# Modulation products on VectorE, a shorter block substitution, paired key products and a gate bound behind solve steps

## The chip, the cores and the metric

The kernel runs on one core of a Trainium2 chip. A core has a matrix engine (TensorE, PE in the profile, with its weight loads shown as PEld), a vector engine (VectorE, DVE), an engine for activations (ScalarE, ACT), a general one (GpSimd, POOL) and a queue engine (SyncE, SP), which here issues most of the transfers. The metric is the time on the device in microseconds of one execution, lower is better.

## The reference, cut to what matters

Two blocks follow each other on 256 tokens of width 1024, all in float32. The first has two layers (a mixer of banded attention and a gated scan, then a mixer with three groups of four scan heads). The second has two layers, each a mixer with a gated delta rule and a sparse attention, and a feed-forward: dense in layer 0, eight experts in layer 1. What the change touches:

```python
mod = c_act @ w_ada[l] + b_ada[l]            # one row of 1024 times 1024 x 6144
sh_m, sc_m, g_m, sh_f, sc_f, g_f = split(mod, 6)
h = rms_norm(x, norm_mix[l]) * (1.0 + sc_m) + sh_m
proj = h @ w_in[l]                           # q, k, v, z, ..., m_g (2048 wide)
...
kb = kc * bc[..., None]                      # delta rule, 8 heads of 64
lower = where(strict, einsum('nbhcd,nbhsd->nbhcs', kb, kc) * decay, 0.0)
tinv = triangular_solve(eye + lower, eye, lower=True, unit_diagonal=True)
...                                          # o_a from tinv, v, decay
gate_a, gate_b = split(sigmoid(m_g), 2)
y = (gate_a * y_a + gate_b * y_b) @ w_out[l]
x = x + g_m * y
```

## The kernel before, in words

**Weights.** Every projection goes through `lin_fm` (line 263, columns of the weight on the output's partitions) or `lin_tm` (277). For each block of 256 columns `wload` (210) loads a raw tile `wr` of 1 MB by a transfer on SP's queue (two buffers), and `wtile` (223) splits it in two halves of 128x1024: ACT writes the high part `wh`, DVE the remainder `wl` (three buffers each). `mm3` (256) then issues three matmuls a product: high by high, high by low, low by high. A block with eight row tiles is 48 matmuls, into one of three PSUM buffers `pl`; an epilogue (`epi`) empties it. `pm` has two PSUM buffers and `pn` three.

**The order.** The program is written once, engine by engine order is made by a planner that lists the instructions by its estimate of when each is ready, with the program's order as rank. So matmuls of a later projection can fill waits of an earlier chain, as far as buffers allow; buffers are handed out in program order. `behind(ins, prev)` orders an instruction after another one on the same engine without a semaphore.

**The stages.** `layer_ab` (0 to some 230 us), `layer_c` (to 525), mixer 0 (to some 838), `ffn_dense` (to some 1100), mixer 1 (to 1378 and the last product with `w_oa_2`), `moe` (to the end).

**Modulation.** For layer 0 of the second block, `ada` (713) makes one of six rows of 1024 per call: eight loads `adaw` of 512 KB on SP's queue (two buffers), 32 matmuls of the column `c_act` against them, in four column groups side by side (64 records in the trace, since a float32 matmul shows as two), an addition of the bias and a transfer on POOL's queue to `modd` in DRAM. `layer_c` calls it at its start (460) and between two projections of its third head group (510), mixer 0 at its start (846), twice ahead of the gates (882) and once behind them (900). `prep_mod` (769) reads rows of `modd` back. For layer 1, `ada_dve` (738) makes the rows on DVE, as chunks behind the weight splits of `ffn_dense`.

**Mixer.** `mixer` (833) projects to `tm`, then queries, keys, values and `z`; `nsa` and `heads` are the sparse attention (their score products `nkT`,`nqT` are written in pairs of heads); `delta` (909) prepares the delta rule. Its loop over eight heads (951 to 979) builds the decays `dd`, multiplies keys by keys and queries (`p0` for the first 128 tokens, `p_1` for the second, on the 64 partitions of a head), and DVE writes them with factors into `UA0` and `UA1` (tiles `dUA`). The 16x16 diagonal blocks go by transfers to `Ub`, 15 pairs of small DVE operations invert them (985 to 989, tiles `dtp` and `dWb`), transfers on ACT's queue lay them out (991 to 996), and `inv32` (1009) makes inverses of 32x32, one half at a time (tiles `dtf`, `dul`, `dys`). `solve` (1027) then goes through eight steps of 32 tokens. A step subtracts the products of all earlier steps' results `X` with the blocks of the key products and multiplies by the inverse:

```python
if T == 0:   # steps 0 to 3
    lst.append((A0(h)[0:32 * cc, 1, r], X[0:32 * cc, 0, xc]))
else:        # steps 4 to 7
    lst.append((A0(h)[:, 1, 128 + 32 * cc:160 + 32 * cc], X[:, 0, xc]))
    if cc:
        lst.append((UA1[0:32 * cc, h, 1, r], X[0:32 * cc, 1, xc]))
```

(per head h; line 1058). Behind the solve in program order stand `gate(1)` and `gate(0)` (897, 898; 1024 columns each, four blocks), the projections `w_ob_2` (901) and `w_oa_2` (906). The planner moves the gates' matmuls ahead of and between the steps of the solve.

Of the kernel before, what the change touches and what calls it, by code (L numbers as in the profile page):

```python
# [89 lines left out]
class Net:  # L90
    def __init__(self, ctx, tc, a, out, dump=None):
# [9 lines left out]
        self.hook = self.hold = None  # L101
# [161 lines left out]
    def lin_fm(self, X, w, c0, ncols, KT, epi):  # L263
# [189 lines left out]
    def layer_c(self):  # L453
        nc, tc, a = self.nc, self.tc, self.a
        with ExitStack() as cx:
# [4 lines left out]
            self.ada()  # L460
# [23 lines left out]
            for gr in range(3):  # L484
# [24 lines left out]
                if gr == 2:  # L509
                    self.ada()  # L510
# [188 lines left out]
    def ada_init(self):  # L699
# [5 lines left out]
        self.ada_next, self.par, self.hook = 0, {}, None  # L705
# [5 lines left out]
        self.modd = [self.dp.tile([6, 4, 256], F32, name="modd%d" % l) for l in range(2)]  # L711

    def ada(self, n=1):

        nc = self.nc
        for _ in range(n):
            r = self.ada_next
            self.ada_next += 1
            w = self.a["w_ada_2"][0]
            ps = self.pl.tile([128, 512], F32, name="pl")  # L720
            o = self.ada_bias(self.aw, 0, r)
            for k in range(8):
                raw = self.aw.tile([128, 1024], F32, name="adaw")
                nc.sync.dma_start(out=raw, in_=w[k * 128:k * 128 + 128, r * 1024:(r + 1) * 1024])
                for j in range(4):
                    self.mm(ps[32 * j:32 * j + 32, :256], self.cs[:, k:k + 1].to_broadcast([128, 32]),
                            raw[:, j * 256:(j + 1) * 256], k == 0, k == 7)
            self.tt(o, o, ps[:, :256], OP.add)
            nc.gpsimd.dma_start(out=self.modd[0][r], in_=o[0::32, :])
# [103 lines left out]
    def mixer(self, l):  # L833
        nc, tc, a = self.nc, self.tc, self.a
        with ExitStack() as cx:
# [9 lines left out]
            if l == 0:  # L845
                self.ada()
# [34 lines left out]
            if l == 0:  # L881
                self.ada(2)
            mg = [p0.tile([128, 8, 256], F32, name="mg%d" % i, tag=("dq", "mg")[i]) for i in range(2)]

            def gate(i):
                self.lin_fm(X, w, 3368 + i * 1024, 1024, 8, lambda m, ps: self.sig(mg[i][:, m:m + 2, :], ps))
# [11 lines left out]
            gate(0)  # L898
            if l == 0:
                self.ada()  # L900
# [8 lines left out]
    def delta(self, l, p1, p2, dq, dv, tm, z):  # L909

        nc, tc, a = self.nc, self.tc, self.a
        c = self.c
# [38 lines left out]
        for h in range(8):  # L951
            hp, r = h // 2, slice(64 * (h % 2), 64 * (h % 2) + 64)
            gt = p2.tile([128, 2, 128], F32, name="dgt")
            for T in range(2):
                self.ts(gt[:, T, :], c["gt"], g[:, T, h:h + 1], None, OP.mult)
            pe = self.pm.tile([128, 4, 128], F32, name="pm")
            self.mm(pe[:, 0:2, :], gt[:, 0, :], c["le1"].rearrange("p (a b) -> p a b", a=2), True, False, **f)
            self.mm(pe[:, 1, :], g[:, 1, h:h + 1].to_broadcast([128, 128]), le, False, False, **f)
            self.mm(pe[:, 2, :], gt[:, 1, :], le, False, False, **f)
            self.mm(pe[:, 0, :], self.identb, self.negst, False, False, **f)  # L960
            self.mm(pe[:, 2, :], self.identb, self.negst, False, True, **f)
            dd = p2.tile([128, 3, 128], F32, name="ddd")
            self.act(dd, pe[:, 0:3, :], AF.Exp)
            p0 = self.pm.tile([128, 2, 256], F32, name="pm")
            p_1 = self.pm.tile([128, 2, 128], F32, name="pm")
            k = dq[r, 4 + hp, :]
            self.mm(p0, k[:, 0:128], dq[r, hp::4, :])
            self.mm(p_1, k[:, 128:256], dq[r, hp::4, 128:256])
            d0 = dd[:, 0:2, :].rearrange("p a b -> p (a b)")
            self.stt(A0(h), p0, be[:, 0, h:h + 1], d0[:, None, :].to_broadcast([128, 2, 256]), OP.mult, OP.mult)  # L970
            self.stt(UA1[:, h], p_1, be[:, 1, h:h + 1], dd[:, 2:3, :].to_broadcast([128, 2, 128]), OP.mult, OP.mult)

            bd = p1.tile([128, 2, 8, 16], F32, name="dbd")
            for T in range(2):
                self.tt(bd[:, T], U(h, T).rearrange("p (b j) -> p b j", j=16), b16, OP.mult)
            nc.vector.tensor_reduce(out=cb[:, :, h], in_=bd.rearrange("p t b j -> p t j b"), op=OP.add, axis=AX)
            for T in range(2):
                q = 64 * T + 8 * h
                nc.gpsimd.dma_start(out=Ub[q:q + 8].rearrange("p s j -> p (s j)"), in_=cb[:, T, h, :])
# [47 lines left out]
    def solve(self, p1, p2, dv, z, A0, UA1, W32, dn, b64, inv32):  # L1027
# [9 lines left out]
        X = p1.tile([128, 2, 512], F32, name="dX", tag="dv")  # L1037
        Rt = p1.tile([128, 512], F32, name="dRt", tag="cbl")
        for n in range(8):
# [8 lines left out]
            for q in range(2):  # L1048
                cq = slice(q * 256, q * 256 + 256)
                src = V[:, 0, :]  # L1050
                if n:
                    for h in range(4 * q, 4 * q + 4):
                        xc = slice(h * 64, h * 64 + 64)
                        lst = []
                        if T == 0:
                            lst.append((A0(h)[0:32 * cc, 1, r], X[0:32 * cc, 0, xc]))
                        else:
                            lst.append((A0(h)[:, 1, 128 + 32 * cc:160 + 32 * cc], X[:, 0, xc]))
                            if cc:
                                lst.append((UA1[0:32 * cc, h, 1, r], X[0:32 * cc, 1, xc]))  # L1060
                        for i, (lh, rh) in enumerate(lst):
                            self.mm(pq[q][r, (h % 4) * 64:(h % 4) * 64 + 64], lh, rh, i == 0, i == len(lst) - 1)
                    self.tt(Rt[r, cq], V[r, T, cq], pq[q][r, :], OP.subtract)
                    src = Rt
                for h in range(4 * q, 4 * q + 4):
                    xc = slice(h * 64, h * 64 + 64)
                    self.mm(pq[q][r, (h % 4) * 64:(h % 4) * 64 + 64], W32[r, T * 8 + h, :], src[r, xc])
# [243 lines left out]
    def ffn_dense(self, l, Y):  # L1311
        nc, tc, a = self.nc, self.tc, self.a
        with ExitStack() as cx:
# [4 lines left out]
            self.tags = {}  # L1318
            mod, scf = self.prep_mod(l, 2, 4, 1)
# [585 lines left out]
```

## Time and profile before

| what | value |
|---|---|
| three runs | 2429.27, 2436.19, 2440.11 us, median 2436.19 |
| the profiled execution | 2426.55 us, span from first to last instruction 2424.7 us |
| mean granted TensorE clock | 0.975 of full |
| PE busy | 2298.4 us, 95% of the span |
| DVE busy | 1565.7 us, 65% |
| ACT busy | 1282.5 us, 53% |
| POOL busy | 388.7 us, 16% |

Busy shares are means over stages with different limits. Matmuls are pipelined, so the time of one record overlaps the next: a record of 0.28 us may follow 0.12 us after the one before it. The clock is given as a share of 2.4 GHz; 0.50 is 1.2 GHz.

### The profile page before, as it was taken

The numbers are of one execution on the slowest core, as the hardware profiler recorded it, in microseconds if no ns is written. First come the engines' busy times: TensorE is split into PE (matmuls) and PEld (weight loads), VectorE is DVE, ScalarE is ACT, GpSimd is POOL, SyncE is SP. The second block draws the span as 40 slices with busy tenths as digits, with TensorE's granted clock in tenths as the row PEclk, the third lists the DMA queues.
The fourth block names the chain that finished last, engine by engine and source line by source line (L and its number), as shares of the span: only waits on it lengthen the run. The fifth ranks groups of instructions, "written<-read, shape, count | busy, mean of one in ns | idle before, by whom it ended". The sixth has DMA issues, their size and how long they took to land. (4 is left out here: it accounts for less than half of the span.)

```text
span 2424.7 us, 40558 instructions
## 1 busy us (share of the span) xinstructions
PE 2298.4 (95%) x15959; PEld 1875.3 (77%) x15959; DVE 1565.7 (65%) x2353; ACT 1282.5 (53%) x1944; POOL 388.7 (16%) x358
## 2 busy tenths in 40 slices
PE   8998999989999899999999999999899999999987
PEld 7887888878678799998878788888788888644333
DVE  5855877757763667676965369998888888511011
ACT  4654666546554444445755258778677867410010
POOL 3201221221110100001110022322331234000000
PEclk9999999989999999999999699999999999999999
DMA  6455446454444578875323358889898999999997
GB/s 202 152 136 162 157 138 205 146 186 135 152 143 140 169 261 282 274 269 156 112 66 106 130 201 323 329 304 363 319 333 323 352 333 337 370 377 408 408 408 317
DMA packets 275192, 586.92 MB, mean 242 GB/s; under 512 B 30752, under 2 KB 171296, under 8 KB 262704
## 3 DMA queue, kind: packets, MB, share of 16 engines
q1 hardware_dynamic: 260688, 577.28, 66.8%
q0 software_dynamic: 5504, 5.91, 1.4%
q8 instruction: 127, 2.08, 0.3%
q10 hardware_dynamic: 8800, 1.05, 0.3%
q14 instruction: 73, 0.60, 0.1%
HBM read 582.26 MB, written 1.64 MB: 241 GB/s over the span
## 5 line engine op out<-in xcount | busy, mean ns | idle before, releaser
L152 DVE TENSOR_TENSOR wl<-wr,wh 128x1024 fp32r<-128x1024 f32 (+3 forms) x733 | 886.3, 1240 | 310.8 <-ACT wh L149 303.6
L149 ACT ACTIVATE wh<-wr 128x1024 fp32r<-128x1024 f32 (+3 forms) x792 | 773.2, 1006 | 414.5 <-PE pl L172 204.6
L172 PE MATMUL pl<-xTh,wh 128*128 128x256 f32 x1696 | 483.5, 286 | 11.1 <-ACT wh L149 5.2
L172 PE MATMUL pl<-xTh,wl 128*128 128x256 f32 x1696 | 480.0, 285 | 0.1
L172 PE MATMUL pl<-xTl,wh 128*128 128x256 f32 x1696 | 479.5, 283 | 0.5 <-DVE xTl L158 0.5
L172 PE MATMUL pl<-wh,eg 128*128 128x448 f32 x1280 | 373.5, 369 | 2.3 <-ACT es L149 2.3
L172 PEld LDWEIGHTS pl<-xTh,wh 128*128 128x128 f32 x1696 | 322.1, 190 | 23.4 <-issue 8.8
L172 PEld LDWEIGHTS pl<-xTl,wh 128*128 128x128 f32 x1696 | 322.5, 190 | 8.0 <-issue 6.8
L172 PEld LDWEIGHTS pl<-xTh,wl 128*128 128x128 f32 x1696 | 321.3, 190 | 6.7 <-issue 5.3
L155 POOL TENSOR_TENSOR wl<-wr,wh 128x896 fp32r<-128x896 f32 (+1 forms) x59 | 189.9, 3219 | 490.3 <-ACT wh L149 383.5
L172 PEld LDWEIGHTS pl<-wh,eg 128*128 128x128 f32 x1280 | 242.4, 190 | 25.0 <-ACT es L149 3.4
L172 PE MATMUL pl<-wl,eg 128*128 128x448 f32 x640 | 238.0, 372 | 14.4 <-POOL wl L155 12.8
L172 PE MATMUL pl<-wr,egf 128*64 128x448 f32 x768 | 163.5, 550 | 3.1 <-DMA wr<-in_w_moe_dram 2.7
L172 PEld LDWEIGHTS pl<-wl,eg 128*128 128x128 f32 x640 | 121.4, 190 | 32.1 <-POOL wl L155 16.9
L172 PEld LDWEIGHTS pl<-wr,egf 128*64 128x64 f32 x768 | 57.8, 137 | 85.6 <-issue 69.7
L172 PE MATMUL pn<-wl,eah 128*128 128x512 f32 x280 | 112.6, 402 | 5.6 <-DVE wl L152 4.1
L172 PE MATMUL pn<-wh,eal 128*128 128x512 f32 x280 | 110.2, 393 | 0.0
L168 DVE TENSOR_SCALAR esu<-pl 128x448 f32<-128x448 f32 x24 | 20.3, 919 | 123.2 <-PE pl L172 123.2
L149 ACT ACTIVATE ehf<-pm 128x448 f32<-128x448 f32 x12 | 6.5, 543 | 168.8 <-PE pn L172 152.0
L172 PE MATMUL pn<-wr,ehf 128*64 128x512 f32 x336 | 89.9, 620 | 5.0 <-DMA wr<-in_w_moe_dram 3.6
L172 PE MATMUL pn<-wh,eah 128*128 128x512 f32 x280 | 89.9, 394 | 0.0
L149 ACT ACTIVATE es<-pl 128x448 f32<-128x448 f32 x64 | 56.9, 989 | 57.8 <-PE pl L172 57.5
(626 smaller groups left out, 3711.9 us busy)
## 6 DMA issues: line engine op xcount, KB each, us to landing
wr<-in_w_moe_dram SPq DMA_DIRECT2D x256, 896.0 KB, 7.0
wr<-in_w_moe_dram SPq DMA_DIRECT2D x96, 1024.0 KB, 8.3
wr<-in_w_dense_dram SPq DMA_DIRECT2D x42, 1024.0 KB, 7.0
wr<-in_w_in_dram SPq DMA_DIRECT2D x32, 1024.0 KB, 5.2
wr<-in_w_in_c_dram SPq DMA_DIRECT2D x30, 1024.0 KB, 5.2
adaw<-in_w_ada_dram SPq DMA_DIRECT2D x48, 512.0 KB, 4.4
adar<-in_w_ada_dram SPq DMA_DIRECT2D x48, 512.0 KB, 5.6
wr<-in_w_in_ab_dram SPq DMA_DIRECT2D x16, 1024.0 KB, 5.3
```

Source lines behind the costliest of these rows:

```text
L149: return self.nc.scalar.activation(out, in_, f, **k)
L152: return self.nc.vector.tensor_tensor(out=out, in0=a, in1=b, op=op)
L155: return self.nc.gpsimd.tensor_tensor(out=out, in0=a, in1=b, op=op)
L168: return self.nc.vector.tensor_scalar(out, a, s1, None, op0=op0)
L172: return self.nc.tensor.matmul(out=out, lhsT=l, rhs=r, start=start, stop=stop, **k)
```

## The change

Four edits.

1. The six modulation rows of layer 0 are made on DVE, by a generator `ada_first` in place of `ada`: 96 chunks of 128x512, each a load of 256 KB and one DVE operation into `adacc`. One chunk is taken up behind the first split of every weight tile from the start of `ada_init` on; what is left is issued at the start of `ffn_dense`. After the 16 chunks of a row, four matmuls with ones (8 records) sum over the partitions.
2. The loop over heads in `delta` goes by pairs: the `p0` products of two heads are issued one after the other, on partitions 0 to 63 and 64 to 127 and into two PSUM tiles, then their `p_1` products.
3. The products with `A0` of steps 4 to 7 of the solve are made once, behind step 3, as eight products of 128x128x64 that are subtracted from `V[:, 1]`.
4. The first matmul of each of the four blocks of `gate(0)` is ordered behind the last matmul of the solve's steps 3, 4, 5 and 6 (the third to the sixth, n = 2 to 5), in both mixers.

```diff
@@ wtile
+            if self.hook0 and k == 0:
+                self.ada_prev = iv
+                next(self.hook0, None)
@@ mm3
-        self.mm(out, ah, bh, start, False, skip_group_check=True)
+        i = self.mm(out, ah, bh, start, False, skip_group_check=True)
+        self.behind(i, self.mm_after)
+        self.mm_after = None
@@ lin_fm(self, X, w, c0, ncols, KT, epi, after=())
+                        if k0 + k == m == 0 and after:
+                            self.mm_after = after.pop(0)
@@ layer_c, mixer: each self.ada() is removed
@@ ada_init
+        self.hook0, self.ada_prev = self.ada_first(), None
+    def ada_first(self):
+        w, o0 = self.a["w_ada_2"][0], None
+        for r in range(6):
             o = self.ada_bias(self.aw, 0, r)
+            acc = self.aw.tile([128, 1024], F32, name="adacc", bufs=1)
             for k in range(8):
+                for h in range(2):
+                    raw = self.aw.tile([128, 512], F32, name="adaw")
+                    c = slice(h * 512, h * 512 + 512)
+                    self.nc.sync.dma_start(out=raw, in_=w[k * 128:k * 128 + 128, r * 1024 + h * 512:r * 1024 + h * 512 + 512])
+                    if k == 0:
+                        i = self.ts(acc[:, c], raw, self.cs[:, 0:1], None, OP.mult)
+                    else:
+                        i = self.stt(acc[:, c], raw, self.cs[:, k:k + 1], acc[:, c], OP.mult, OP.add)
+                    self.behind(i, self.ada_prev)
+                    if k == 7 and h == 1:
+                        ps = self.pl.tile([128, 512], F32, name="pl")[:, :256]
+                        for j in range(4):
+                            self.mm(ps[32 * j:32 * j + 32], self.one.to_broadcast([128, 32]),
+                                    acc[:, j * 256:(j + 1) * 256])
+                        self.tt(o, o, ps, OP.add)
+                        self.nc.gpsimd.dma_start(out=self.modd[0][r], in_=o[0::32, :])
+                    yield
@@ mixer
-            gate(0)
+            gate(0, self.steps[2:6])
@@ delta
-        for h in range(8):
...
-            self.mm(p0, k[:, 0:128], dq[r, hp::4, :])
-            self.mm(p_1, k[:, 128:256], dq[r, hp::4, 128:256])
+        for hp in range(4):
...
+            p0 = [self.pm.tile([128, 2, 256], F32, name="pm") for _ in range(2)]
+            for i, r in enumerate(rows):
+                self.mm(p0[i], dq[r, 4 + hp, 0:128], dq[r, hp::4, :])
...
+            p_1 = [self.pm.tile([128, 2, 128], F32, name="pm") for _ in range(2)]
+            for i, r in enumerate(rows):
+                self.mm(p_1[i], dq[r, 4 + hp, 128:256], dq[r, hp::4, 128:256])
@@ solve
-                src = V[:, 0, :]
-                if n:
+                src = V[:, T, :]
+                if cc:
...
+                        u = A0(h)[0:32 * cc, 1, r] if T == 0 else UA1[0:32 * cc, h, 1, r]
+                        self.mm(pq[q][r, (h % 4) * 64:(h % 4) * 64 + 64], u, X[0:32 * cc, T, xc])
...
+            self.steps.append(last)
...
+            if n == 3:
+                ps = self.pbank()
+                for q in range(2):
+                    cq = slice(q * 256, q * 256 + 256)
+                    for h in range(4 * q, 4 * q + 4):
+                        xc = slice(h * 64, h * 64 + 64)
+                        self.mm(ps[:, xc], A0(h)[:, 1, 128:256], X[:, 0, xc])
+                    self.tt(V[:, 1, cq], V[:, 1, cq], ps[:, cq], OP.subtract)
@@ ffn_dense
+            for _ in self.hook0:
+                pass
+            self.hook0 = None
             mod, scf = self.prep_mod(l, 2, 4, 1)
```

## Rows read from the trace of the kernel before

**Rows 1.** The page's head: the span and its instructions.
```profile
span 2424.7 us, 40558 instructions
```
**Rows 2.** Waits of PE over the span: us in total, times, longest us.
```profile
PE pl L172 <- DMA adaw<-in_w_ada_dram: 13.4, 5, 5.7
```
**Rows 3.** By stage, adaw on PE: stretch, length, busy (records), PEclk, DMA share, GB/s.
```profile
200.00:480.00 280.00, 10.48 (x128) 0.99 0.53 172
480.00:525.00 45.00, 6.02 (x64) 0.89 0.64 205
```
**Rows 4.** The same view in mixer 0, ahead of its solve and in it.
```profile
525.00:729.00 204.00, 12.65 (x128) 0.98 0.46 141
729.00:800.00 71.00, 6.12 (x64) 0.99 0.43 138
```
**Rows 5.** Timeline of PE: start, duration, operation, records, idle time before and releaser.
```profile
516.25 1.08 PE L172 MATMUL pl<-adaw,adacs 128*32 128x256 f32 x8 [3.03 <-DMA adaw<-in_w_ada_dram]
517.26 2.08 PE L172 MATMUL pn<-ln,kc 128*128 128x256 f32 x4
```
**Rows 6.** Timeline of ACT at mixer 0's start.
```profile
512.20 1.13 ACT L149 ACTIVATE ln<-xf 128x512 f32<-128x512 f32 x2
```
**Rows 7.** By stage, all engines: PE, PEld, DVE, ACT, POOL busy, PEclk, DMA share, GB/s.
```profile
231.00:525.00 294.00, 273.35 (x2569) 240.35 (x2569) 212.20 (x357) 176.88 (x267) 72.78 (x125) 0.97 0.53 171
```
**Rows 8.** Groups by line and form on DVE: count, busy us, mean ns, idle before.
```profile
L158 DVE SCALAR_TENSOR_TENSOR dq<-dq,dsq 128x512 f32<-128x512 f32 x8 | 5.5, 682 | 0.0
```
**Rows 9.** By stretch of 20 us, DVE alone.
```profile
60.00:80.00 20.00, 17.25 (x27) 1.00 0.51 159
...
420.00:440.00 20.00, 17.96 (x29) 1.00 0.59 202
...
620.00:640.00 20.00, 18.24 (x49) 1.00 0.45 137
```
**Rows 10.** By stage, PE: both mixers ahead of the solve and in it.
```profile
525.00:729.00 204.00, 201.73 (x1510) 0.98 0.46 141
729.00:800.00 71.00, 66.05 (x780) 0.99 0.43 138
1106.00:1319.00 213.00, 209.91 (x1535) 0.98 0.35 109
1319.00:1378.00 59.00, 54.74 (x574) 0.72 0.19 58
```
**Rows 11.** Products with tile dUA on PE in both solves.
```profile
729.00:800.00 71.00, 17.92 (x208) 0.99 0.43 138
1319.00:1378.00 59.00, 25.92 (x208) 0.72 0.19 58
```
**Rows 12.** Products with tile xTl (a third of the gates') in both solves.
```profile
729.00:800.00 71.00, 14.06 (x50) 0.99 0.43 138
1319.00:1378.00 59.00, 0.00 (x0) 0.72 0.19 58
```
**Rows 13.** All engines in 15 us of mixer 1's solve.
```profile
1345.00:1360.00 15.00, 14.72 (x98) 8.40 (x94) 3.10 (x6) 2.99 (x7) 0.00 (x0) 0.50 0.00 0
```
**Rows 14.** Timeline of DVE in mixer 1, around the small substitution.
```profile
1278.45 1.23 DVE L152 TENSOR_TENSOR wl<-wr,wh 128x1024 fp32r<-128x1024 f32 x1 [1.06 <-ACT wh L149]
1280.13 0.18 DVE L152 TENSOR_TENSOR dtp<-dUb,dWb 128x15 f32<-128x15 f32 x1
1296.33 0.39 DVE L990 COPY dWb<-dWb 128x256 f32<-128x256 f32 x1
```
**Rows 15.** Timeline of PE in mixer 0: score products of the sparse attention.
```profile
631.38 0.92 PE L172 MATMUL pn<-nkT,nqT 64*128 64x256 f32 x8
639.52 0.92 PE L172 MATMUL pn<-nkT,nqT 64*128 64x256 f32 x4
```
**Rows 16.** Products with tile dq on PE, mixer 0.
```profile
560.00:729.00 169.00, 14.28 (x32) 0.99 0.46 140
```
**Rows 17.** PE in 100 us of the dense feed-forward.
```profile
900.00:1000.00 100.00, 97.73 (x833) 1.00 0.85 285
```

More of the change, by code (lines that the diff above doesn't have):

```diff
@@ L100, in __init__ @@
         self.wp = E(tc.tile_pool(name="wsplit", bufs=3))
-        self.hook = self.hold = None
+        self.hook = self.hold = self.hook0 = self.mm_after = None
         self.wafter, self.moe_on, self.wfirst = None, False, []
@@ L258, in mm3, with lin_fm @@
         (ah, al), (bh, bl) = A, B
-        self.mm(out, ah, bh, start, False, skip_group_check=True)
+        i = self.mm(out, ah, bh, start, False, skip_group_check=True)
+        self.behind(i, self.mm_after)
+        self.mm_after = None
         self.mm(out, ah, bl, False, False, skip_group_check=True)
         return self.mm(out, al, bh, False, stop, skip_group_check=True)
-    def lin_fm(self, X, w, c0, ncols, KT, epi):
+    def lin_fm(self, X, w, c0, ncols, KT, epi, after=()):
+        after = list(after)
         for j in range(0, ncols, 256):
@@ L704, in ada_init @@
         self.tt(self.cs, self.cs, cc, OP.mult)
-        self.ada_next, self.par, self.hook = 0, {}, None
+        self.par, self.hook = {}, None
         lg = self.load_cols(self.ap, a["ln_gain"].rearrange("l (k p) -> (l k) p", p=128), 16, "lng", "cwr")
@@ L711, in ada_init @@
         self.modd = [self.dp.tile([6, 4, 256], F32, name="modd%d" % l) for l in range(2)]
[L713 to L720, printed above, removed]
+        self.hook0, self.ada_prev = self.ada_first(), None
+    def ada_first(self):
+        w, o0 = self.a["w_ada_2"][0], None
+        for r in range(6):
             o = self.ada_bias(self.aw, 0, r)
+            acc = self.aw.tile([128, 1024], F32, name="adacc", bufs=1)
             for k in range(8):
[L723 to L729, printed above, removed]
+                for h in range(2):
[15 more added lines that the diff above has]
+                    yield
     def ada_bias(self, pool, l, r):
@@ L880, in mixer, with gate @@
             oa = solve()
-            if l == 0:
-                self.ada(2)
             mg = [p0.tile([128, 8, 256], F32, name="mg%d" % i, tag=("dq", "mg")[i]) for i in range(2)]
-            def gate(i):
-                self.lin_fm(X, w, 3368 + i * 1024, 1024, 8, lambda m, ps: self.sig(mg[i][:, m:m + 2, :], ps))
+            def gate(i, after=()):
+                self.lin_fm(X, w, 3368 + i * 1024, 1024, 8, lambda m, ps: self.sig(mg[i][:, m:m + 2, :], ps), after)
             def branch_b(m, ps):
@@ L950, in delta @@
         U = lambda h, T: A0(h)[:, 1, 0:128] if T == 0 else UA1[:, h, 1, :]
-        for h in range(8):
[L952 to L966, printed above, removed]
-            self.mm(p0, k[:, 0:128], dq[r, hp::4, :])
-            self.mm(p_1, k[:, 128:256], dq[r, hp::4, 128:256])
[L969 to L979, printed above, removed]
@@ new lines, in delta @@
+        for hp in range(4):
+            dds = []
+            for h in (2 * hp, 2 * hp + 1):
+                gt = p2.tile([128, 2, 128], F32, name="dgt")
+                for T in range(2):
+                    self.ts(gt[:, T, :], c["gt"], g[:, T, h:h + 1], None, OP.mult)
+                pe = self.pm.tile([128, 4, 128], F32, name="pm")
+                self.mm(pe[:, 0:2, :], gt[:, 0, :], c["le1"].rearrange("p (a b) -> p a b", a=2), True, False, **f)
+                self.mm(pe[:, 1, :], g[:, 1, h:h + 1].to_broadcast([128, 128]), le, False, False, **f)
+                self.mm(pe[:, 2, :], gt[:, 1, :], le, False, False, **f)
+                self.mm(pe[:, 0, :], self.identb, self.negst, False, False, **f)
+                self.mm(pe[:, 2, :], self.identb, self.negst, False, True, **f)
+                dd = p2.tile([128, 3, 128], F32, name="ddd")
+                self.act(dd, pe[:, 0:3, :], AF.Exp)
+                dds.append(dd)
+            rows = [slice(64 * i, 64 * i + 64) for i in range(2)]
+            p0 = [self.pm.tile([128, 2, 256], F32, name="pm") for _ in range(2)]
+            for i, r in enumerate(rows):
+                self.mm(p0[i], dq[r, 4 + hp, 0:128], dq[r, hp::4, :])
+            for i in range(2):
+                d0 = dds[i][:, 0:2, :].rearrange("p a b -> p (a b)")
+                self.stt(A0(2 * hp + i), p0[i], be[:, 0, 2 * hp + i:2 * hp + i + 1],
+                         d0[:, None, :].to_broadcast([128, 2, 256]), OP.mult, OP.mult)
+            p_1 = [self.pm.tile([128, 2, 128], F32, name="pm") for _ in range(2)]
+            for i, r in enumerate(rows):
+                self.mm(p_1[i], dq[r, 4 + hp, 128:256], dq[r, hp::4, 128:256])
+            for i in range(2):
+                h = 2 * hp + i
+                self.stt(UA1[:, h], p_1[i], be[:, 1, h:h + 1], dds[i][:, 2:3, :].to_broadcast([128, 2, 128]),
+                         OP.mult, OP.mult)
+            for h in (2 * hp, 2 * hp + 1):
+                bd = p1.tile([128, 2, 8, 16], F32, name="dbd")
+                for T in range(2):
+                    self.tt(bd[:, T], U(h, T).rearrange("p (b j) -> p b j", j=16), b16, OP.mult)
+                nc.vector.tensor_reduce(out=cb[:, :, h], in_=bd.rearrange("p t b j -> p t j b"), op=OP.add, axis=AX)
+                for T in range(2):
+                    q = 64 * T + 8 * h
+                    nc.gpsimd.dma_start(out=Ub[q:q + 8].rearrange("p s j -> p (s j)"), in_=cb[:, T, h, :])
@@ L1037, in solve @@
         X = p1.tile([128, 2, 512], F32, name="dX", tag="dv")
+        self.steps = []
         Rt = p1.tile([128, 512], F32, name="dRt", tag="cbl")
@@ L1066, in solve @@
                     xc = slice(h * 64, h * 64 + 64)
-                    self.mm(pq[q][r, (h % 4) * 64:(h % 4) * 64 + 64], W32[r, T * 8 + h, :], src[r, xc])
+                    last = self.mm(pq[q][r, (h % 4) * 64:(h % 4) * 64 + 64], W32[r, T * 8 + h, :], src[r, xc])
                 self.act(X[r, T, cq], pq[q][r, :])
+            self.steps.append(last)
             if n == 0:
                 inv32(1)
+            if n == 3:
[6 more added lines that the diff above has]
+                    self.tt(V[:, 1, cq], V[:, 1, cq], ps[:, cq], OP.subtract)
             if cc == 3:
```

15 lines of the change are left out of this document (removed).

## The prediction

> **What bounds the kernel now.** The times come from one profiled execution of 2426.55 us, its span 2424.7 us [rows 1]. It lies 9.6 us below the median of the three runs (2436.19), so every sum is made against 2426.55 and 9.6 is added at the end. I read the page first, then the waits of TensorE (PE) in total, then tables by stage of the stretches that the change touches, then timelines at their edges.
>
> PE sets the time. In layer_c and up to mixer 0 it is busy for 273 of 294 us, VectorE (DVE) for 212 [rows 7]; in the mixers PE is busy for 201.7 of 204 and 209.9 of 213 us ahead of the solve, for 66.1 of 71 and 54.7 of 59 in it [rows 10]. So a microsecond taken from PE's work counts in full, unless a chain of small operations ends later or DVE fills up. The change takes modulation and A0 products off PE, and moves a gate from ahead of the solves into them.
>
> **(a) Modulation ahead of mixer 0.** On PE it is six rows of 64 records each: 10.48 + 6.02 us for the three rows that layer_c's code issues [rows 3], 12.65 + 6.12 for three in mixer 0 [rows 4]. PE also waits 13.4 us, five times, for `adaw` transfers, at most 5.7 at once [rows 2]. Not all of that is on the path. At mixer 0's start the last such wait is 3.0 us, and behind its products PE takes the first squares of the layer norm at 517.26 [rows 5]; ACT had made two of them in the 1.13 us from 512.20 on, the first by 512.8 [rows 6]. So 4.4 of the 7.5 us waited there delay the end; the same share of the 5.7 at layer_c's start is 3.3. Of the busy time I count layer_c's row between projections (half of the 10.48, 5.2) and 1.8 at its start; the rest lies where PE would have waited anyway. Gain 7.7 + 7.0 = 14.7.
>
> Against it stand the ones products of three rows, 8 records each: 0.66 us by the 10.48 / 128 of [rows 3], 2.0 in all (3.2 if each group takes the 1.08 of [rows 5]). And 62 of the 96 chunks (24 in layer_ab, 38 in layer_c, one behind each weight tile) go to DVE. The same operation at the same 128x512 takes 0.682 us in delta [rows 8], so that is 42 us, and the 26 in layer_c bring DVE from 212 to 238 of 294 us. A chunk stands behind a weight split; where DVE is full, the next split comes late and PE waits for it. Bounds: 0 if chunks fall only into idle DVE; 11 if each in a full stretch costs its length (of the 23 stretches of 20 us from 60 to 520 six hold over 17 us of DVE work, the first and the last of them in [rows 9], so 16 chunks of 0.68). I take 4, nearer to the lower end, because DVE is idle for 82 of layer_c's 294 us. A chunk also waits for its own transfer at the head of DVE's queue, the next split behind it, and on SP's queue an `adaw` load that waits for one of its two buffers holds back the weight load behind it. The bytes are the same as before and the DMA engines are 0.53 busy [rows 7]: I take nothing, 5 as the bound. **Net -14.7 + 2.0 + 4 = -8** (-13 to +4).
>
> **(b) Mixer 1.** A dense stretch shows 833 matmuls in 97.73 us [rows 17], 0.117 us each; gate(0) is four blocks of 48, 22.5 us. It stands wholly ahead of step 0 now: no X product is left in the solve [rows 12]. Bound behind steps 3 to 6 it leaves the 213 us, which by work alone would lose 22.5. The other limit is the chain from the key products to step 0. Its 30 small substitution operations (0.18 us each, 5.4 bare) take from 1280.13 to 1296.33, among splits of 1.23 us [rows 14]; behind them come transfers, inv32, and step 0 at 1319. gate(0)'s eight splits (9.8 us) leave that stretch too. I take **-18**; bounds -10, if only the splits' time goes, and -22.5.
>
> The solve then resembles mixer 0's of before: 71 us at clock 0.99 with 50 of the gate's 64 triples inside [rows 10, 12]. Add 14 triples (4.9). Take off its modulation row (6.12 with overlaps [rows 4], 5.2 by [rows 3]). Take off what the substitution saves: dUA records are 17.92 / 208 = 0.086 us [rows 11]; 64 go (5.5), 16 come, wider (2.2 at 0.14): -3.3; of the two added subtractions step 4 gives one back. That is 67.4; 1.6 for bare steps 0 to 2 makes 69, **+10** on 59. The clock is inside this: the same 208 records take 25.92 us in mixer 1's solve, granted 0.72, against 17.92 in mixer 0's [rows 11], so a filled solve gives about 8 us back.
>
> One row shows what the clock does: from 1345 to 1360 PE is busy for 14.72 of 15 us with small products, and is granted 0.50, its 1.2 GHz level [rows 13]. The Trainium skill ("TensorE: Matmul & The Clock Gate", Part 1: The HAM clock gate) has the array at half rate by default and after idling, and lets activity release it. Read plainly, that rule would have a PE so busy at full rate, and filling the solve would give nothing back: (b) would be some 8 us worse, with neither gain nor loss. The measurement disagrees and decides, so that way gets no chance of its own.
>
> **Mixer 1: -18 + 10 = -8** (-12.5 to +15, the latter rival C).
>
> **(c) Mixer 0.** Ahead of its solve two modulation rows go (10.5 by [rows 3]) and 14 triples (4.9): by work -15.4. The chain is the same as mixer 1's and DVE gets chunks besides, so I take half, -8 (0 to -15.4). The solve is 71 + 4.9 - 5.2 - 3.3 + 1.6 = 69, -2, and two ones groups come (+1). **-9** (-16 to +2).
>
> **(d) Paired key products.** Two score products on rows 0 to 63 and 64 to 127 run side by side when they are issued next to each other: 8 records in 0.92 us, against 4 alone in the same 0.92 [rows 15]. Key products are 32 records and 14.28 us a mixer [rows 16], so pairing is worth up to 7.1. But the four alone are written as a pair as well: the order on PE is the planner's, and it parts them. I take -1 a mixer (0 to -7): **-2**.
>
> **(e) Into the dense feed-forward.** 92 tiles have passed by then; four chunks (2.7 us), a ones group, and a write and a read of the row through DRAM stand ahead of the first residual. W_out's products go on meanwhile in three PSUM buffers, which cover 3 x 5.6 us. **+1**; 5 if the cover ends early.
>
> Sum: -8 - 8 - 9 - 2 + 1 = -26, so 2400.5, and with 9.6 **2410 us**. With each bound taken half-way the likeliest case lies between 2397 and 2423.
>
> **The rivals.** *A, everything fills.* DVE hides all chunks ((a) -13), mixer 1 is bound by work alone (-22.5 + 10 = -12.5), mixer 0 loses -11, pairs are found (-14), +1: -49.5, 2387 us. For it: PE over 97% busy ahead of both solves. Against: the parted score products, and the chain.
>
> *B, DVE becomes the bound.* The chunks cost their 11 us in full stretches and carry 5 us of the `adaw` wait over to the splits: (a) is -14.7 + 2 + 11 + 5 = +3. Mixer 0, where DVE already has 18.2 of 20 us [rows 9], gives back 6: -3. With -8 and +1 this is -7, 2429 us. For it: the scans that fill DVE are where PE waits for splits already. Against: layer_c's idle DVE.
>
> *C, the other side: slower.* Weight tiles are loaded and split in program order, into two raw and three split buffers. gate(0)'s first tile and half of its second sit there until step 3, ob's weights queue behind them, and nothing wide is left for PE in steps 0 to 2. If the chain and not PE's work sets step 0, the 213 us stay, and the solve is 59 + 22.5 - 3.3 - 8 (clock) + 4 (bare steps, the half of some 8 us that half clock would cost) = 74: +15. Mixer 0 by the same sum +4; with (a) -8 and +1: +12, 2448 us. It decides if step 0 of mixer 1 comes less than 10 us earlier, counted from the mixer's first product. Against it: mixer 0, with 50 triples fewer ahead of its solve, reaches it 9 us sooner [rows 10].
>
> That the change doesn't do what it says, in that the planner parts the pairs, is inside the forecast.
>
> **How the numbers follow.** Forecast 0.52, A 0.16, B 0.21, C 0.11. A measurement of this kernel tells a change of about 0.5% (12 us) from none: faster is below 2424, slower above 2448. Faster are the forecast (but for 0.02), A, and 0.04 of B: 0.70. Slower are 0.08 of C and 0.01 of B: 0.09. The rest, 0.21, is the same. The range leaves out C and half of A, 2387 to 2438.
>
> **What would show it.** (a) PE has no `adaw` wait and takes the squares at mixer 0's start within 1 us of ACT; wrong if its waits for `wl` there grow by over 10 us. (b) Step 0 of mixer 1 comes 195 us after the stretch's start instead of 213, the solve takes 67 to 71 us, its PEclk is over 0.9. (c) dUA records fall from 208 to 160 a mixer, and mixer 0's step 0 comes at 196 instead of 204. (d) dq products appear in fours of about 1.1 us, if paired. A time over 2424 would make the prediction wrong, and the gain ahead of the solves would be the first place to look.

## The result

The changed kernel is slower, by little but beyond the noise. Nine runs have a median of 2449.2 us (2443.9 to 2460.5) against 2437.0 us of the kernel before on the same chip, a ratio of 1.0057 (95% interval 1.0039 to 1.0074); on another chip it was 1.0069 (1.0047 to 1.0091). 2410 was forecast, with 2387 to 2438 as the range.

The head of the page after: the span, the busy times, the granted clock in 40 slices.

```profile
span 2453.6 us, 39943 instructions
PE 2295.7 (94%) x15527; PEld 1887.0 (77%) x15527; DVE 1625.2 (66%) x2449; ACT 1281.2 (52%) x1944; POOL 402.8 (16%) x358
PEclk9998999999978899999997989999999999999999
```

The granted clock before, from the same place of its page:

```profile
PEclk9999999989999999999999699999999999999999
```

PE lost 432 records and only 2.7 us of busy time, while the span grew by 29 (this profiled execution, 2455.3 us, lies 6 above its median, that of before 10 below). The clock has fallen in the 12th to 14th slice of 61 us, which hold the last part ahead of mixer 0's solve, the solve and its end: 0.7 and 0.8, where the kernel before had 0.9.

Two profiled executions of either kernel (the second ones are runs of the study below), cut at the first product of each mixer and at the first product with `w_oa_2`, in us:

| stage | before | after | mean difference | forecast |
|---|---|---|---|---|
| both layers of the first block | 525.1, 530.3 | 524.7, 529.4 | -0.7 | -8 |
| mixer 0, to its `w_oa_2` | 274.6, 279.7 | 279.1, 272.3 | -1.5 | -9 |
| from there to mixer 1 (`W_out`, dense feed-forward) | 303.6, 304.0 | 315.3, 322.1 | +14.9 | +1 |
| mixer 1, to its `w_oa_2` | 274.8, 278.5 | 276.6, 276.7 | 0.0 | -8 |
| from there to the end (`W_out`, experts) | 1046.7, 1048.3 | 1057.9, 1053.6 | +8.3 | 0 |

Nothing was gained where gains were forecast, and the loss lies behind the mixers, in stretches to which the forecast gave one microsecond. (The pairing's -2 stands inside the mixers.) The column adds up to +21, more than the +12 to +17 of the medians, because both profiled executions of the changed kernel lie 5 to 6 us above their medians.

What answers to [rows 10], PE by stage in the mixers, ahead of the solve and in it (columns as there):

```profile
525.00:731.00 206.00, 198.93 (x1352) 0.92 0.39 121
731.00:804.00 73.00, 68.50 (x735) 0.88 0.32 106
1119.00:1324.00 205.00, 195.69 (x1342) 0.91 0.33 101
1324.00:1396.00 72.00, 69.88 (x727) 0.89 0.25 81
```

Mixer 1's solve is full now (0.89 instead of 0.72), as forecast, but its forerun (the stretch from the mixer's first product to step 0) has fallen from 0.98 to 0.91 and is 9 us less busy than it is long. What answers to [rows 11], products with tile dUA, and to [rows 12], tile xTl, in the two solves:

```profile
731.00:804.00 73.00, 15.18 (x160) 0.88 0.32 106
1323.00:1396.00 73.00, 15.40 (x160) 0.88 0.25 80
```

```profile
731.00:804.00 73.00, 19.00 (x64) 0.88 0.32 106
1324.00:1396.00 72.00, 19.10 (x64) 0.89 0.25 81
```

The substitution has the 160 records that were forecast, and all 64 triples of the gate stand in either solve. The key products ([rows 16]) gained nothing:

```profile
560.00:732.00 172.00, 16.55 (x32) 0.90 0.35 106
```

32 records take 16.55 us instead of 14.28. (The last ones fall into the stretch of lower clock; in mixer 1 they take 14.55 us in both kernels.) No pair ran side by side. In mixer 1 the first pair's two `p0` products, on PE:

```profile
1225.72 1.12 PE L172 MATMUL pm<-dq 64*128 64x512 f32 x2
1229.21 1.12 PE L172 MATMUL pm<-dq 64*128 64x512 f32 x2
```

They are written one after the other and issued 3.5 us apart. Where the planner happened to leave two `p0` products together, once in mixer 1 of `f1_early` (a run of the study below), the four records took the time of two:

```profile
1259.21 1.13 PE L172 MATMUL pm<-dq 64*128 64x512 f32 x4
```

**The entry to the dense feed-forward.** The queue SP, then PE, in the changed kernel's mixer 0 behind the solve:

```profile
803.84 0.43 SPq L219 DMA_DIRECT2D wr<-in_w_out_dram  x1
804.50 0.77 SPq L730 DMA_DIRECT2D adaw<-in_w_ada_dram  x1
814.13 0.38 SPq L219 DMA_DIRECT2D wr<-in_w_out_dram  x1
814.80 3.23 SPq L730 DMA_DIRECT2D adaw<-in_w_ada_dram  x2
822.23 0.38 SPq L219 DMA_DIRECT2D wr<-in_w_out_dram  x1
```

```profile
824.27 0.75 PE L172 MATMUL pl<-adacc,kc 128*32 128x256 f32 x4 [4.87 <-DVE adacc L158]
847.56 0.36 PE L172 MATMUL pl<-xTh,wh 128*128 128x256 f32 x1 [3.07 <-DVE xf L158]
```

In PE's order the ones products of the leftover chunks stand ahead of `W_out`'s. They wait 4.87 us for the third of the four chunks, and `W_out`'s first product follows them at 824.9, though its first operands had been ready since 814. On SP's queue each leftover `adaw` load goes out when a chunk frees a buffer, and `W_out`'s loads stand between them, 8 to 10 us apart. What that order costs by itself isn't shown: before the change the same four loads were 5 to 19 us apart, each released by a split as here. The row then goes through DRAM, and PE waits another 3.07 us for the first residual, which needs it.

**The start of `W_out` in mixer 1.** PE, ACT and SP of the changed kernel, and SP of the kernel before:

```profile
1415.60 0.58 PE L172 MATMUL pl<-xTh,wh 128*128 128x256 f32 x1 [7.29 <-ACT wh L149]
```

```profile
1414.49 2.00 ACT L149 ACTIVATE wh<-wr 128x1024 fp32r<-128x1024 f32 x2 [3.60 <-DMA wr<-in_w_out_dram]
```

```profile
1392.92 2.51 SPq L219 DMA_DIRECT2D wr<-in_w_out_dram  x3
1395.47 4.70 SPq L219 DMA_DIRECT2D wr<-in_w_moe_dram  x2
1400.27 1.55 SPq L219 DMA_DIRECT2D wr<-in_w_out_dram  x1
```

```profile
1337.08 40.55 SPq L219 DMA_DIRECT2D wr<-in_w_out_dram  x4
```

Before, the first of `W_out`'s four tiles was loaded at 1337, during the solve. Now gate(0) holds the buffers until step 6, and ob's and w_oa's tiles follow one by one. `W_out`'s loads begin at 1392.92, and one of the four goes out at 1400.27, behind two loads for the experts. ACT waits for that one, and PE waits 7.29 us for ACT.

**Ahead of step 0.** All engines in the last 39 us before mixer 1's step 0 (PE, PEld, DVE, ACT, POOL, PEclk, DMA share, GB/s), before and after:

```profile
1280.00:1319.00 39.00, 38.20 (x395) 31.61 (x394) 22.93 (x78) 21.98 (x48) 0.00 (x0) 1.00 0.35 95
```

```profile
1285.00:1324.00 39.00, 33.28 (x306) 23.54 (x305) 24.97 (x90) 18.09 (x47) 5.28 (x8) 0.77 0.26 69
```

With gate(0) bound there is nothing wide left, PE is idle for 5.7 of 39 us and granted 0.77. So it is no longer PE's work that sets the time there; the chain of small operations to step 0 is what remains. (`f2_ob_first`, with 72 wide products more ahead of it, reaches step 0 at 205.3 us after the mixer's first product, the changed kernel at 204.6.)

**The layers' starts.** PE and ACT at mixer 0's start, to set beside [rows 5, 6]; then all engines in [rows 7]'s stretch, and the chunks on DVE by form:

```profile
516.41 2.08 PE L172 MATMUL pn<-ln,kc 128*128 128x256 f32 x4 [6.29 <-ACT ln L149]
```

```profile
515.75 1.13 ACT L149 ACTIVATE ln<-xf 128x512 f32<-128x512 f32 x2
```

```profile
231.00:525.00 294.00, 268.96 (x2439) 242.84 (x2439) 238.73 (x396) 176.88 (x269) 78.33 (x123) 0.95 0.53 170
```

```profile
L158 DVE SCALAR_TENSOR_TENSOR adacc<-adaw,adacs,adacc 128x512 f32<-128x512 f32 x84 | 66.3, 794 | 7.5 <-DMA adaw<-in_w_ada_dram 7.3
```

PE takes the squares 0.1 us behind ACT's first, as said. But ACT makes them at 515.75 instead of 512.20: the delay of 4.4 us is gone and 3.5 us of it was used up before. DVE has 238.7 us there, as worked out (238), and the clock fell from 0.97 to 0.95.

A chunk with an addition takes 0.794 us on average, not the 0.682 of [rows 8], and that could have been read before. The operation of [rows 8] multiplies by a constant; a chunk reads its factor from a tile (`adacs`), one value a partition. An operation of that kind and shape stood in the same view of the kernel before:

```profile
L158 DVE SCALAR_TENSOR_TENSOR dUA<-pm,dbe,ddd 128x512 f32<-128x512 f32 x16 | 12.0, 749 | 9.8 <-PE pm L172 9.8
```

79 of the 84 chunks take 0.729 to 0.754; four take 1.58 to 1.79, and those aren't explained.

### The profile page after: what moved, and what is told of

Its sections match the earlier page's. It is cut to its first block, busy times and chain, and to the rows that moved or that the text cites. A ratio compares the mean times of both kernels' runs of the same rounds, so it can differ in the third digit from the quotient of the medians.

```text
span 2453.6 us, 39943 instructions
## 1 busy us (share of the span) xinstructions
PE 2295.7 (94%) x15527; PEld 1887.0 (77%) x15527; DVE 1625.2 (66%) x2449; ACT 1281.2 (52%) x1944; POOL 402.8 (16%) x358
## 5 line engine op out<-in xcount | busy, mean ns | idle before, releaser
L172 PE MATMUL pl<-xTh,wh 128*128 128x256 f32 x1696 | 490.1, 290 | 21.5 <-ACT wh L149 12.3
L172 PE MATMUL pl<-xTl,wh 128*128 128x256 f32 x1696 | 486.4, 287 | 1.2 <-DVE xTl L152 0.9
L172 PEld LDWEIGHTS pl<-xTh,wl 128*128 128x128 f32 x1696 | 325.5, 192 | 12.9 <-issue 6.8
L172 PE MATMUL pl<-wl,eg 128*128 128x448 f32 x640 | 238.0, 372 | 15.5 <-POOL wl L155 12.5
L172 PE MATMUL pl<-wr,egf 128*64 128x448 f32 x768 | 162.6, 550 | 4.3 <-DMA wr<-in_w_moe_dram 4.2
```

What stands on the lines that cost most here:

```text
L172: return self.nc.tensor.matmul(out=out, lhsT=l, rhs=r, start=start, stop=stop, **k)
```

## The experiments

Theory 1, from the two traces: the binding costs, by a chain that then sets step 0, by half clock, and by weights that queue behind the bound gate. Theory 2: the chunks on DVE cost. Ratios are to the kernel before, run beside on the same chip, with 95% intervals.

**The parts alone.** `e1_unbound` takes the binding away, `e2_mod_pe` puts the modulation back on PE, `e3_delta_only` does both, `e4_mod_only` leaves the modulation on DVE alone.

```diff
-            gate(0, self.steps[2:6])     # e1, e3, e4
+            gate(0)
```

(e2 and e3 have `ada` and its calls of the kernel before in place of `ada_first`; e4 has its `delta` loop and `solve`.)

> The changed kernel without the binding of gate(0): modulation on VectorE, shorter substitution and pairs stay. Theory 1 (the binding is what costs: chain-bound pre-solves, half clock in bare steps, weights of ob, oa and W_out no longer loaded ahead): 2425 to 2432 us, 5 to 12 below before; the 7.3 us wait at the start of mixer 1's W_out is gone, mixer 1 from its first product to its first oa product is about 271 instead of 276.6. Theory 2 (the chunks on VectorE are what costs): 2444 to 2450 as the changed kernel, since they are still there.

Measured: 2433.0 us, 0.9989 (0.9972 to 1.0005).

> The changed kernel with the modulation rows back on TensorE as before (binding, shorter substitution and pairs stay). Theory 1: 2440 to 2450 us, no better than the changed kernel, with the W_out wait of about 7 us still there; the wait of 4.9 us for adacc at the start of the dense feed-forward is gone. Theory 2: 2425 to 2432.

Measured: 2451.2 us, 1.0067 (1.0051 to 1.0082).

> The kernel before with the shorter substitution and the paired key products alone. By the measured solve (dUA records 160 instead of 208) 3 us a mixer: 2428 to 2434 us under both theories; if the pair order delays the last key product by itself (it came 15 us later in mixer 0 of the changed kernel), 2437 to 2445.

Measured: 2433.4 us, 0.9988 (0.9975 to 1.0002).

> The kernel before with the modulation on VectorE alone. Theory 1: layer starts 4 us shorter each, entry to the dense feed-forward 6 to 9 longer, mixer 0 some 5 shorter: 2430 to 2437 us. Theory 2: 2443 to 2450.

Measured: 2437.4 us, 1.0011 (0.9997 to 1.0026).

Theory 1's ranges held for e3 and were missed by about 1 us or less in e1, e2 and e4; theory 2's were missed by 6 to 19 us. (Mixer 1 of e1 took 265.7 us, shorter than the 271 expected; e4's layers were not shorter.) The binding costs 1.0057 - 0.9989 = 0.0068 with the modulation on DVE and 1.0067 - 0.9988 = 0.0079 without it, 17 and 19 us: theory 1. The modulation as written is worth nothing (1.0011), the shorter substitution and the pairs some 3 us that the interval doesn't tell from none. The parts add up: 0.0011 - 0.0012 + 0.007 is 0.007. Ahead of mixer 1's step 0, e1 has what the kernel before had:

```profile
1288.00:1327.00 39.00, 39.00 (x400) 32.09 (x399) 25.41 (x82) 23.52 (x53) 0.00 (x0) 1.00 0.40 109
```

**What in the binding costs.** `f1_early` binds the blocks to steps 1 to 4; `f2_ob_first` keeps the binding and puts ob's projection ahead of gate(0); `f4_bind_m1` binds in mixer 1 alone.

```diff
-            gate(0, self.steps[2:6])
-            self.lin_fm(ob, a["w_ob_2"][l], 0, 1024, 4, branch_b)
+            gate(0, self.steps[0:4])     # f1, ob unmoved
...
+            self.lin_fm(ob, a["w_ob_2"][l], 0, 1024, 4, branch_b)     # f2
+            gate(0, self.steps[2:6])
...
+            gate(0, self.steps[2:6] if l else ())     # f4, ob unmoved
```

> The changed kernel with gate(0)'s four blocks bound behind steps 1 to 4 of the solve instead of 3 to 6. Theory 1a (the lost ahead-loading costs: ob, oa and W_out weights queue behind gate(0) in the buffers, so the end of the mixer starves): the gate ends two steps earlier, W_out is loaded ahead again, 2437 to 2443 us, W_out's wait below 3 us. Theory 1b (bare small products at half clock ahead of the gate cost): also better, PEclk of the solve up, 2437 to 2443, but with W_out's 7 us wait still there. Theory 1c (the pre-solve's chain costs, wherever the gate is put afterwards): unchanged, 2446 to 2452.

Measured: 2444.1 us, 1.0018 (0.9996 to 1.0040), 1 us above the range of 1a. `W_out`'s wait is gone, yet the last 39 us ahead of mixer 1's step 0 are barer still than with the late binding:

```profile
1286.00:1325.00 39.00, 31.51 (x266) 20.19 (x264) 21.91 (x88) 15.66 (x49) 1.98 (x4) 0.64 0.18 42
```

So the late weights are about half of the binding's price (1.0057 to 1.0018, with intervals that just touch), and the bare forerun is not cured by an earlier gate.

> The changed kernel with the projection of ob placed ahead of gate(0) in program order, so that it no longer queues behind the bound gate in the weight buffers; binding unchanged. Theory 1a or 1b: ob's 192 products stand in or ahead of steps 0 to 2, the mixer's end loses some 17 us of products, W_out's wait stays or shrinks a little: 2432 to 2440 us. Theory 1c: ob fills the pre-solve or the bare steps, some gain too, 2440 to 2446.

Measured: 2432.6 us, 0.9985 (0.9962 to 1.0009). The whole price of the binding is gone. Both its halves are treated: ob's products (96, not 192; 72 of them ahead of step 0 in either mixer) fill PE, and the weight loads run ahead again, so that `W_out`'s wait, which was expected to stay, is gone too. All engines ahead of step 0, and SP behind the solve, in this kernel:

```profile
1277.00:1316.00 39.00, 36.96 (x374) 29.41 (x373) 24.89 (x88) 19.45 (x49) 5.76 (x8) 0.91 0.31 83
```

```profile
1347.77 20.85 SPq L219 DMA_DIRECT2D wr<-in_w_oa_dram  x4
1372.55 7.81 SPq L219 DMA_DIRECT2D wr<-in_w_out_dram  x4
1380.41 16.52 SPq L219 DMA_DIRECT2D wr<-in_w_moe_dram  x7
```

All four `W_out` loads now precede the experts'. The run doesn't part the two halves, since one move treats both. More split buffers, which would have parted them, were not tried.

> The changed kernel with the binding in mixer 1 alone. If both mixers pay alike: 2440 to 2443 us. If it is the late W_out of mixer 1 and the experts' loads behind it: 2445 to 2450. If mixer 0 pays: 2433 to 2437.

Measured: 2440.2 us, 1.0016 (0.9996 to 1.0035): about half-way between e1 and the changed kernel. By the times alone mixer 0 pays (1.0016 against 1.0057 and 1.0069); mixer 1's share, 1.0016 against 0.9989, lies within overlapping intervals, and the profiles have to show it.

They do. Four pieces, in the profiles of all sixteen runs, in us:

| piece | range | in which kernels |
|---|---|---|
| mixer 1, to its `w_oa_2` | 273.1 to 278.9 | bound in mixer 1, ob behind the gate (after, h2, e2, f1, f4, g2) |
| | 262.5 to 271.5 | unbound with any of the other edits (e1, e3, e4, f3, h1, h3), and ob ahead (f2, g1) |
| from there to the first expert's product | 66.8 to 68.5 | bound behind steps 3 to 6 in mixer 1, ob behind (after, h2, e2, f4, g2) |
| | 58.0 to 59.2 | all eleven others, f1 and the kernel before among them |
| mixer 0's `w_oa_2` to the first dense product | 80.1 to 83.3 | chunks left over (after, h2, e1, e4, f1, f2, f4) |
| | 68.0 to 73.6 | none left over, or the modulation on PE |
| from there to mixer 1 | 231.5 to 244.5 | no order by edit |

The kernel before takes 274.8 and 278.5 for mixer 1. So binding in mixer 1 costs 9 us at `W_out`, and it forgoes some 8 us in the mixer that the unbound kernels gain.

**What eats the modulation's gain.** `f3_no_left` is e1 with one more chunk behind every sixth weight tile, so that the last row is done some ten tiles ahead of the dense feed-forward. `h1_no_left_again` is the same kernel, `h2_after_again` the changed one, `h3_mod_no_left` is e4 with the same edit.

```diff
                 next(self.hook0, None)
+                self.h0 = getattr(self, "h0", 0) + 1
+                if self.h0 % 6 == 0:
+                    next(self.hook0, None)
```

> The changed kernel without the binding and with one more modulation chunk behind every sixth weight tile, so that none is left for the start of the dense feed-forward. If the 4.9 us wait for adacc and the 3.1 us wait for the residual there are what eats the modulation's gain: 2424 to 2428 us, 8 below the unbound kernel. If another work ends last there: 2431 to 2435.

Measured: 2418.0 us, 0.9914 (0.9882 to 0.9946), better than either text.

> The unbound kernel without leftover chunks once more, beside the changed kernel on one chip. If its 0.9914 was exact: 2410 to 2420 us, 0.989 to 0.994. If the leftovers are worth no more than in the bound kernel (0.0018 between 1.0057 and 1.0039): 0.996 to 0.999.

Measured: 2419.7 us, 0.9939 (0.9915 to 0.9963). Of the two texts the one with 0.989 to 0.994 held.

> The changed kernel once more, so that both ends stand on one chip: 1.004 to 1.008. Its profile shows again how far the stages lie from one execution to the next: the dense feed-forward 313 to 318 us if the leftovers set it, not 300 to 305.

Measured: 2450.6 us, 1.0069 (1.0047 to 1.0091); the stretch to mixer 1 322.1 us, above the 313 to 318 expected.

> The kernel before with the modulation on VectorE alone and no chunk left over. If the leftovers ate the gain of the modulation: 0.993 to 0.997, as its sibling with leftovers was 1.0011 and the dense feed-forward loses 13 us. If the chunks cost as much in the layers as they save: 0.999 to 1.002.

Measured: 2423.2 us, 0.9953 (0.9934 to 0.9972).

Four chunks of 0.8 us at the wrong place cost 0.0058 with the modulation alone (1.0011 to 0.9953), and 0.0050 to 0.0075 in the unbound kernel: 12 to 18 us. The stretch from mixer 0's `w_oa_2` to mixer 1 is 318.0 us in e4 and 318.3 in e1, 305.0 in h3 and 304.8 in f3. (The length of the whole stretch doesn't prove it: e3, with no chunk at all, takes 313.6. Its excess lies behind the first dense product; up to there e3 takes 69.1 and e4 80.9, h3 68.0.) The waits of PE there (total, times, longest), in e4 and in h3:

```profile
PE pl L172 <- DVE adacc L158: 4.4, 1, 4.4
PE pl L172 <- ACT oah L149: 4.0, 1, 4.0
PE pl L172 <- DVE xf L158: 3.1, 1, 3.1
```

```profile
PE pl L172 <- ACT oah L149: 3.0, 1, 3.0
PE pl L172 <- ACT xTh L149: 2.1, 1, 2.1
```

The two waits, for `adacc` and for `xf`, are 7.5 of the 13 us. The ones products take 1.1, and behind either wait PE works at a lower clock. Stretches of 6 us behind the two waits in e4, and one amid `W_out`'s products in h3 (all engines):

```profile
820.00:826.00 6.00, 6.00 (x40) 5.72 (x37) 3.93 (x7) 1.69 (x2) 0.00 (x0) 0.72 0.39 125
844.00:850.00 6.00, 6.00 (x41) 6.00 (x40) 1.62 (x3) 1.97 (x3) 2.55 (x2) 0.72 0.01 3
```

```profile
824.00:830.00 6.00, 6.00 (x53) 6.00 (x53) 3.14 (x4) 2.62 (x4) 0.85 (x1) 1.00 0.83 275
```

That is 25 records fewer, 2.9 us at 0.117. Together 11.5 of the 12.9 us are accounted for.

**Both repairs.** `g2_bound_no_left` is the changed kernel with the last edit; `g1_both` has ob ahead as well. `g4_before_again` is the kernel before.

> The changed kernel, binding and order as they are, with one more chunk behind every sixth weight tile, so that none is left. If leftovers and binding cost independently: 1.0057 less 0.0075, 0.998, 2428 to 2436 us. If the leftovers only mattered in the unbound kernel: 2445 to 2452.

Measured: 2443.4 us, 1.0039 (1.0023 to 1.0056), outside both texts. Its stretch to mixer 1 is 300.2 us, so the stage was mended here too. The profiled execution is 15 us shorter than that of the changed kernel, but it lies 3 below its median and the other 6 above; the medians differ by 6 to 7. Why a stage shorter by 15 to 22 gives 6 to 7 in the bound kernel stays open.

> The changed kernel with both repairs: ob's projection ahead of the bound gate(0), and one more modulation chunk behind every sixth weight tile so that none is left for the dense feed-forward. If the two effects add: 0.9985 less 0.0075, 0.991, 2412 to 2420 us; if binding has a worth of its own once ob is out of its way: below the unbound kernel without leftovers (0.9914), 2404 to 2412. If the extra chunks on VectorE hurt the chain that then sets step 0: 2425 to 2432.

Measured: 2425.7 us, 0.9959 (0.9941 to 0.9977). That is better than the kernel before and than g2; against f2 (0.9985) and the unbound kernel without leftovers (0.9914, 0.9939) the intervals overlap. A binding whose two costs are treated shows no worth here. The time is in the range of the third text, but its cause isn't seen: step 0 of the mixers comes 207.7 and 204.7 us after their first products, in f2 206.9 and 205.3.

> The kernel before once more, for a second profile: the stages from mixer 0's last projection to mixer 1 and from mixer 1's to the end tell how far one profiled execution of the same program lies from another. Theory: 5 us or more in the two feed-forward stages, under 2 in the layers and mixers.

Measured: 2442.8 us. The expectation was the wrong way round: the feed-forward stages repeat within 2 us (303.6 and 304.0, 1046.7 and 1048.3), the layers and mixers differ by 4 to 5. In the changed kernel the same two stages differ by 6.8 and 4.3, so +14.9 and +8.3 in the table of the result are outside what two executions differ by, but not far; the two parts of them that the edits move, in the table of the four pieces, repeat within 2 us. The differences in the mixers are not outside.

The version to keep is the unbound one without leftovers: 0.9914 and 0.9939 on two chips, 14 to 21 us below the kernel before.

## Why the prediction was wrong

**(e), the border to the dense feed-forward, +1: mis-sized, it measured +15.** The sum took W_out's products as cover for the leftover chunks, by three PSUM buffers. It did not look at what the ones products stand ahead of on PE's own queue. The cover was itself queued behind the thing to be covered, and the lower clock behind two waits came on top. h3 and f3 show it: with no chunk left the stage is back at 305 us and the kernel gains 12 to 18 us.

**(b), mixer 1: the first step failed, the second held.** The forerun was to lose 18 of 216 us (counted from the mixer's first product) and lost 11.5 in either profile; the solve was to grow by 10 and is 72.0 us in both, 13 above one profile of before (58.8) and 10 above the other (62.3). So the sum was 0, where -8 stood. The mechanism was half seen. The chain from the last key product to step 0 did shrink with the gate gone, from 49.4 to 36.0 us; but the last key product itself, which the working took as free to move up with PE's work, came 2.0 us later than before (168.6 after the mixer's start, 166.6 before). Work-bound by the busy share, chain-bound in fact: PE was 98% busy because the planner had wide work to fill with, and when that went, the stretch emptied (33.3 of 39 us, clock 0.77) more than it shortened. Nor would the -18 have been enough. In e2 and g2, bound alike, the last key product came at 155.7 and 159.1 and step 0 at 200.6 and 198.2, so the forerun did lose 15 to 18 us. Their solves then took 75.2 and 80.7 us and the mixer 275.8 and 278.9, as before the change.

**The term that was missing: weights behind a bound gate, +8 after mixer 1.** Rival C described the mechanism (tiles in program order, the first tile and a half waiting in the buffers, ob's behind them), but priced it only within the solve. Its largest part fell behind the mixer, on `W_out`'s first products. Rival C's time (2448) was met almost exactly and for other reasons: its condition, a step 0 less than 10 us earlier, was not fulfilled in mixer 1, and its +15 and +4 there were 0 and -1.5. That its time fits is luck.

**(c), mixer 0, -9: measured -1.5 +- 5.** Two modulation rows and 14 triples did leave PE ahead of step 0, but the last key product came at 166.8 and 162.6 us after the mixer's start, against 150.7 and 154.2 before. The chunks on DVE do that: in e4, with nothing else changed, it is 162.2, and in e3, with the modulation on PE, 150.7. "Half of what the work says" had no row behind it; the DVE row of that stretch, 18.2 of 20 us, stood under rival B.

**(a), the layers, -8: measured -0.7 +- 5.** The delay at mixer 0's start was read rightly and is gone, but the layer norm ahead of it came 3.5 us later, probably from DVE work in layer_c (not traced step by step; PE's waits for `wl` from 60 to 505 us rose from 5.4 to 8.8). At layer_c's start nothing was gained: PE now waits 3.6 us for a small load and reaches its first projection at 238.5 instead of 238.0, so the 5.7 us wait for `adaw` had lain beside the layer norm's chain altogether, and "the same share" of it was a guess. The rest is rival B in small: a chunk's 0.794 us, where the sum had the 0.682 of an operation with a constant factor, and waits on DVE. Where the modulation's gain without leftovers (0.0047 by h3) comes from is not fully placed: h3's layers take 525.2 us, its mixer 0 273.7, and 270.8 of mixer 1, whose text is unchanged there, against 274.8 and 278.5. In mixer 1 of h3 the planner put 14 of gate(0)'s 64 triples and all of ob's products behind step 0, where before it put none of the gate's and 86 of ob's 96 there; e3 and e4 are alike. That an order which it finds anew is part of each result is likely, and wasn't tested by itself.

**(d), the pairs, -2 and the shorter substitution, -3.3 a mixer.** The substitution has its 160 records, as forecast. (The 0.14 us for each of its 16 wide products had no row behind it; the 16 take 2.1 us, where 2.2 stood.) No pair was found in the changed kernel, and so none of the -2. Together the two edits are 0.9988, some 3 us that may be none, where 8.6 stood.

**The clock.** A full solve did get its clock back in mixer 1: 0.89 instead of 0.72, and the dUA records cost there what they cost in mixer 0 (15.40 and 15.18 us for 160). What wasn't weighed is that it is paid ahead of the solve, by a forerun that went from 0.98 to 0.91. The forerun's last 39 us are idle for 5.7, at most 1.45 at a time, and granted 0.77: 1.00 up to 1305.9, just behind the longest of these gaps, and 0.50 from there into the solve. [Rows 13] has 0.50 at 98% busy. The Trainium skill ("TensorE: Matmul & The Clock Gate", Part 1: The HAM clock gate) has idling bring the half rate back: by that rule the forerun, where idling came ahead of the fall, agrees and [rows 13] does not.

## What to carry to other kernels

A busy share of 98% doesn't say that a stretch is bound by that work: look at which chain would be left if the work went, and how early its first link can move. Ordering wide work late also orders late everything that takes its buffers after it, so price the next projections' loads, not only the stretch. Leftovers of a background job, flushed at a stage's border, stand ahead of the new stage's work on the engines that they use; finish them before it (ten tiles were enough here). Take an operation's price from a row with the same operands, not only the same name and shape.

## What was not expected of the hardware

Of two vector operations of the same name and shape (128x512), the one whose factor comes from a tile took 0.742 to 0.749 us on average, the one with a constant factor 0.68: `dUA<-pm,dbe,ddd` and `xf<-pm,esrt,xf` against `dq<-dq,dsq` and `xf<-xf,pl`, in the kernel before.

Between 1392.9 and 1400.3 six loads of 0.9 to 1 MB were issued in the changed kernel, four for `W_out` and two for the experts. The first landed after 5.8 us; the last, `W_out`'s of 1400.27, after 14.1, just before ACT started on it at 1414.49. The mixers' input weights, of the same size, have a median of 5.1 us on the same page.
